# Splitting a load of weights with one instruction per engine, with rings of six places, and a bias table held for two heads at a time

## The chip, the cores and the metric

The kernel runs on one core of a Trainium2 chip. The metric is the device time of one execution in microseconds (us). The program before took 847.29, 847.55 and 848.8 us in three runs; the median is 847.55 us. Lower is better.

## What is computed

A hybrid encoder of two layers, for 256 tokens of width 1024, in float32. Of the reference, cut to what matters here:

```python
def _token_mixer(xn, w_in, w_pool, pool_scale, w_a, w_b, w_o, rel_bias):
    u, q, k, v, g_pool, g_attn = jnp.split(xn @ w_in, SPLITS, axis=-1)
    ...                                   # pooled: centred means of u minus u, by group
    pool_out = jnp.einsum('bsgc,gcd->bsgd', pooled, w_pool).reshape(B, S, POOL_WIDTH) * pool_scale
    ...
        logits = einsum(q, k) * scale + bias      # 4 heads in each of 3 groups, rel_bias by distance
        p = exp(logits - lse); o = einsum(p, v)   # the groups joined by the softmax of lse
    ...
    merged = sigmoid(g_pool) * (pool_out @ w_a) + sigmoid(g_attn) * (attn_out @ w_b)
    return merged @ w_o

def _conv_ffn(xn, w_up, conv_w, conv_b, w_down):
    a, gval = jnp.split(xn @ w_up, 2, axis=-1)
    a = conv(a) + conv_b                          # depthwise, width 3
    return (jax.nn.gelu(a) * gval) @ w_down

def reference(...):
    h = x
    for layer in range(DEPTH):
        h = h + _token_mixer(_rmsnorm(h, norm1[layer]), ...)
        h = h + _conv_ffn(_rmsnorm(h, norm2[layer]), ...)
    return _rmsnorm(h, norm_f)
```

Nearly all of the arithmetic is products of the 256 tokens with weight matrices that are read once from memory (186 MB are read in all).

## The kernel before

**Weights.** Each product of f32 operands a and w is made of three matmuls on values of a shorter mantissa (fp32r): first part of a by first part of w, first part of a by rest of w, rest of a by first part of w. So each weight is split on the chip. The class Weights does it. A *load* is one DMA of 1 MB (128 partitions x 2048 f32) on SP's queue (L178) into one of three places of `raw`. A load has two *pieces* of 128x1024. For each piece ACT casts the first part `wh` (L259) and DVE subtracts it from `raw` to give the rest `wl` (L261). wh and wl have rings of five places (BUFS = 5), one piece each; a place comes free when PE's last matmul on the piece is done. PE takes 12 matmuls of 128x512 for a piece. `get` hands PE the next piece and first opens pieces up to LOOK = 3 (4 in stretches that are ordered by hand) ahead, as far as the ring has places, and asks for further loads. Some pieces go to other tiles ("slots") or, in the first layer's start, are scaled by a gain while they are split.

**Order.** Each engine works through its instructions in the order in which they were issued. In most of the kernel that order is the one of the calls in the code, so a cast or subtraction that isn't ready holds up what was issued behind it on the same engine. SP issues the DMAs in the same manner, and a DMA that must wait for its data holds up the DMAs behind it.

**The scores.** In the middle of each layer, while PE makes the gates' and the pool's products (t_ps), the four heads hh = 0 to 3 of attention are done between them, by a table of steps (`steps`). `scores(hh)` issues PE's matmuls s_ps, then on DVE an addition of the bias with the running minimum (L1351, reads s_ps and `bt`), on ACT the exponential (L1361), on DVE the reciprocal, on ACT the scaling (L1368), on DVE two transposes (L852). The result is turned around through memory: one DMA writes it (L857, `turning`) and four DMAs read it back (L864, `turned_p`), which `W.bring_back` issues one or more steps later. `turn(hh)` splits what came back into `pth` (ACT, L1378) and `ptl` (DVE, L1379), and `weigh(hh)` issues PE's o_ps from pth, ptl and the values (L1388), followed by the parts at2 (ACT L1397, DVE L1398). `keep_gated` (DVE L1410) makes `pa` from th (ACT L1483) and t_ps. The table of steps has scores(0) at 3, bring_back and scores(1) at 4, bring_back at 5, turn(0) and scores(2) at 7, weigh(0), bring_back and turn(1) at 8, scores(3) at 9, weigh(1) at 10, turn(2) at 12, weigh(2) at 13.

**The bias.** `build_bias`, in layer 0, spreads rel_bias over distances, puts it into memory (`fd`), and reads it back with five DMAs (L559) of 256 KB into `bt`, a constant tile of 128 x 4 heads x 640 f32, where it stays for both layers.

**The products by seven.** One block of w_up in each layer, between the MLP's groups (order `BLOCK`, lines L917 for the matmuls), and in layer 1 also some of the values (order `VALUES`) are done with seven products in place of eight (Strassen's manner): the quadrants 11, 12, 21, 22 of the weight, and sums T1 to T4 of them that DVE makes in place in `raw` (L344, two instructions of 128x1024 for each sum, each issued behind the split of a half that it needs). A sum T2 needs T1 and quadrant 22, T3 needs T2, T4 needs quadrant 21. In BLOCK a "d" stands for a piece of w_down, which PE takes in between (res_ps, L715 to L717). ACT copies banks between the products: L1681 after 11, L1685 after T1 (the "fifth" product, copied from the bank that product 22 then adds to), L1688 after 22.

Of the kernel before, what the change touches and what calls it, by code (L numbers as in the profile page):

```python
# [16 lines left out]
P = 128  # L17
# [39 lines left out]
VALUES = {  # L57
# [5 lines left out]
}  # L63
SUMS = {"22": "T2", "T2": "T3", "21": "T4"}
HALVES = (slice(0, 512), slice(512, D))
# [53 lines left out]
class Weights:  # L119
# [3 lines left out]

    RAW, BUFS, LOOK = 3, 5, 3

    def __init__(self, tc, pool, idle, small):
        self.tc, self.nc, self.pool, self.idle, self.small = tc, tc.nc, pool, idle, small
        self.loads, self.pieces = [], []  # L130
        self.n_loaded, self.n_split, self.n_got = 0, 0, 0
        self.raw, self.split = {}, {}
        self.live = set()
        self.behind, self.later = (), []
        self.last, self.rests = [None, None], {}
        self.between = []
# [3 lines left out]
        self.sums = {}  # L140

    def add(self, src, shape, cuts, tag=None):

        n = len(self.loads)
        self.loads.append((src, shape, tag))
        return [(n, cut, c_shape) for cut, c_shape in cuts]

    def use(self, pieces, slots=()):
        slots = list(slots) + [None] * len(pieces)
# [58 lines left out]
    def _split(self, upto):  # L208
        nc = self.nc
        first = self.n_split  # L210
        while self.n_split < len(self.pieces):
            i = self.n_split
            n, cut, shape, slot = self.pieces[i]
            if i >= upto and (slot is None or i >= max(upto, first + 2) or i >= upto + 4 or i < 4):
                break
            if slot is None and len(self.live) == self.BUFS:
                break
            self.load(n + 1)
            with ExitStack() as queued:
                for insts, some in self.later:  # L220
                    for inst in insts if i in some else ():
                        if not self.by_hand:
                            queued.enter_context(self.tc.issue_after(inst.ins))
                for hi, lo, *_ in self.open_next():
# [12 lines left out]
    def open_next(self):  # L237


        nc, i = self.nc, self.n_split  # L240
        n, cut, shape, slot = self.pieces[i]
        if slot is None:
            self.live.add(i)
            h, l = (
                self.pool.tile([P, *shape], F32R, tag=tag, bufs=self.BUFS, name=f"{tag}{i}")
                for tag in ("wh", "wl")
            )
        else:
            tag, part, of = (*slot, 0, 1)[:3]
            if part == 0:  # L250
                self.shared = self.idle.tile([P, of, 2, *shape], F32R, tag=tag, name=f"{tag}{i}")
            h, l = self.shared[:, part, 0], self.shared[:, part, 1]
        src = cut(self.raw[n])
        self.split[i] = (h, l)
        self.n_split += 1
        if i >= self.n_scaled:
            def make(n):
                if n == 0:
                    inst = nc.scalar.copy(out=h, in_=src)  # L259
                else:  # L260
                    inst = self.rests[i] = nc.vector.tensor_sub(out=l, in0=src, in1=h.bitcast(F32))  # L261
# [17 lines left out]

        return [scaled(j) for j in range(shape[0])]  # L280
# [10 lines left out]

    def free(self, i):
        self.live.discard(i)


@with_exitstack
def encoder(ctx, tc, x, w_in, w_pool, pool_scale, w_a, w_b, w_o, norm1, norm2, w_up, conv_w,
# [32 lines left out]
    def use_block(units, made, first):  # L330
# [6 lines left out]
        def raw(name, j):  # L337
            return W.raw[made[name][0][0]][:, 2 * j : 2 * j + 2]

        def sum_later(i, name, j):  # L340

            def make():
                one, other = terms[name]
                nc.vector.tensor_sub(out=raw(name, j), in0=raw(one, j), in1=raw(other, j))  # L344

            W.sums[i] = make

        for j in range(2):
            sum_later(len(W.pieces) + first + j, "T1", j)
        behind = [u for u in units if len(u) > 2]  # L350
        for unit in units:
            if len(unit) > 2:
                W.use([unit])
                behind = behind[1:] or behind
                continue
            name, j = unit
            if name in SUMS:
                sum_later(len(W.pieces), SUMS[name], j)
            if name in ("22", "21"):
                W.use([made[name][j]])  # L360
            else:
                W.use([(behind[0][0], lambda t, name=name, j=j: raw(name, j), (2, 512))])

    def first_quadrants(w, n):
        return {
# [158 lines left out]

        return turn

    bt = const.tile([P, HPG, NT * P], F32, name="bt")

    def build_bias():

# [22 lines left out]

        fd = dram.tile([1, HPG * NT * 256], F32, name="fd")
        nc.sync.dma_start(out=fd[0].rearrange("(h e) -> h e", h=HPG), in_=fsb)
        yield
        for blk, kind in enumerate((4, 3, 1, 0, 2)):
            src = bass.AP(fd.tensor, fd.offset + kind * 256, [[1, P], [NT * 256, HPG], [1, P]])
            nc.sync.dma_start(out=bt[:, :, blk * P : (blk + 1) * P], in_=src)  # L559
        yield  # L560
# [560 lines left out]
    for l in range(DEPTH):  # L1121
# [282 lines left out]
        def keep_gated(n):  # L1404
# [362 lines left out]
```

## Time and profile before

| | |
|---|---|
| median of three runs | 847.55 us |
| the profiled execution | 848.11 us |
| its span | 846.3 us |
| PE (matmul) | 99% busy |
| DVE (VectorE) | 79% busy, 860 instructions |
| ACT (ScalarE) | 63% busy, 770 instructions |
| SP's DMAs | 147,480 packets, 212.67 MB, 76.8% of 16 engines |
| granted TensorE clock | 1.00 of full speed in the stretches shown |

The profile is of one execution. A row of a timeline gives the start and the length in us, the engine, the line of the code, the operation, what it writes and reads (names without buffer numbers), sizes, and how often it ran in a row; a bracket at the end is idle time of the engine ahead of it and what ended that. SPq is SP's DMA queue: its row is the issue of a transfer, and not the transfer itself. A row of waits gives the engine and line that waited, for what, the us in total, the number of times and the longest. A row of windows gives, for a stretch of time, the busy us of PE, PE's weight loads, DVE, ACT and POOL with the number of instructions, then the granted clock, the share of the DMA engines and the GB/s. Matmuls overlap in the rows: a 128x512 one is listed with 0.39 us while the next starts 0.227 us later.

### The profile page before, as it was taken

How to read it: one execution, taken by the hardware profiler on the slowest of the kernel's cores; microseconds unless marked ns; L12 is line 12 of the kernel's file. 1: busy time of each engine (PE TensorE's matmuls, PEld its weight loads, DVE VectorE, ACT ScalarE, POOL GpSimd, SP SyncE). 2: the span in 40 equal slices, each digit the busy share in tenths (PEclk: the TensorE clock that was granted, in tenths of full speed). 3: DMA queues.
4: the chain of work that ended last, by engine and by line, in shares of the span. 5: the costliest groups of instructions: out<-in, count | busy, mean ns of one | idle time of the engine just before them, and what ended most of it. 6: DMA issues, size and time to landing. Idle time of an engine off the chain costs nothing.

```text
span 846.3 us, 10959 instructions
## 1 busy us (share of the span) xinstructions
PE 838.7 (99%) x3889; PEld 699.3 (83%) x3889; DVE 665.5 (79%) x860; ACT 531.1 (63%) x770; POOL 35.5 (4%) x96
## 2 busy tenths in 40 slices
PE   9999999999999999999999999999999999999997
PEld 7888888888888887888888888888888888888886
DVE  6968877757767799788898997868577867998884
ACT  7744556655554776488765555577455647757883
POOL 1720000000010000000000000000000100000000
PEclk9999999999999999999999999999999999999999
DMA  8699987796759886889857669968777499768861
GB/s 305 211 304 289 317 282 251 246 282 218 233 206 302 276 275 199 256 264 316 272 185 225 222 225 316 284 235 261 247 261 269 164 308 309 227 224 275 303 218 50
DMA packets 147967, 214.02 MB, mean 253 GB/s; under 512 B 7801, under 2 KB 69185, under 8 KB 147913
## 3 DMA queue, kind: packets, MB, share of 16 engines
q1 hardware_dynamic: 147480, 212.67, 76.8%
q10 hardware_dynamic: 432, 0.66, 0.2%
q8 instruction: 30, 0.49, 0.2%
q14 instruction: 25, 0.20, 0.1%
HBM read 186.02 MB, written 27.28 MB: 252 GB/s over the span
## 4 chain that ended last, share of the span: by engine, by line
PE 90%; DMA 3%; DVE 3%; ACT 2%; issue 1%; POOL 0%; ACTq 0%; SPq 0%; DVEq 0%; POOLq 0%
PE t_ps L798 54%; PE res_ps L716 6%; PE res_ps L715 6%; PE res_ps L717 6%; PE t_ps L917 4%; PE v_ps L798 3%; DMA raw<-in_w_up_dram 3%; PE v_ps L1101 3%; PE v_ps L917 2%; PE pool_ps L702 1%; PE v_ps L1000 1%; PE o_ps L1392 1%; PE s_ps L1344 1%; ACT wh L259 1%; DVE wl L261 1%; PE s_ps L1339 1%
## 5 line engine op out<-in xcount | busy, mean ns | idle before, releaser
L261 DVE TENSOR_TENSOR wl<-raw,wh 128x1024 fp32r<-128x1024 f32 x292 | 350.9, 1219 | 92.4 <-ACT wh L259 91.7
L798 PE MATMUL t_ps<-wh,x 128*128 128x512 f32 x1280 | 401.8, 390 | 0.0
L259 ACT CAST wh<-raw 128x1024 fp32r<-128x1024 f32 x292 | 302.1, 1048 | 158.8 <-PE t_ps L798 71.2
L798 PEld LDWEIGHTS t_ps<-wh,x 128*128 128x128 f32 x1280 | 240.3, 188 | 50.0
L798 PE MATMUL t_ps<-wl,x 128*128 128x512 f32 x640 | 249.0, 389 | 0.0
L798 PEld LDWEIGHTS t_ps<-wl,x 128*128 128x128 f32 x640 | 120.2, 188 | 24.7
L715 PE MATMUL res_ps<-wh,actq 128*128 128x512 f32 (+1 forms) x184 | 70.0, 380 | 0.0
L716 PE MATMUL res_ps<-wl,actq 128*128 128x512 f32 (+1 forms) x184 | 69.8, 380 | 0.0
L717 PE MATMUL res_ps<-wh,actk 128*128 128x512 f32 (+1 forms) x184 | 69.3, 380 | 0.0
L798 PE MATMUL t_ps<-wh,po 128*128 128x512 f32 x128 | 41.4, 395 | 0.0
L715 PEld LDWEIGHTS res_ps<-wh,actq 128*128 128x128 f32 x184 | 34.6, 188 | 6.7
L716 PEld LDWEIGHTS res_ps<-wl,actq 128*128 128x128 f32 x184 | 34.6, 188 | 6.7
L717 PEld LDWEIGHTS res_ps<-wh,actk 128*128 128x128 f32 x184 | 34.6, 188 | 6.5
L1604 ACT ACTIVATE a<-zga,prm 128x256 f32<-128x256 f32 x80 | 38.9, 512 | 0.0
L592 POOL TENSOR_SCALAR ss<-ss 128x1 f32<-128x1 f32 x8 | 3.1, 386 | 764.2 <-ACT junk L585 764.2
L344 DVE TENSOR_TENSOR raw<-raw,raw 128x1024 f32<-128x1024 f32 x24 | 29.3, 1222 | 0.0
L798 PEld LDWEIGHTS t_ps<-wh,po 128*128 128x128 f32 x128 | 24.0, 188 | 4.9
L715 PE MATMUL res_ps<-wh,m 128*128 128x512 f32 (+1 forms) x72 | 26.5, 368 | 0.0
L716 PE MATMUL res_ps<-wl,m 128*128 128x512 f32 (+1 forms) x72 | 26.3, 365 | 0.0
L717 PE MATMUL res_ps<-wh,m 128*128 128x512 f32 (+1 forms) x72 | 26.0, 365 | 0.0
L1608 DVE TENSOR_TENSOR y<-y,a 128x510 f32<-128x510 f32 x22 | 14.9, 679 | 13.6 <-ACT y L1602 13.6
L798 PE MATMUL t_ps<-wl,po 128*128 128x512 f32 x64 | 24.9, 390 | 0.0
(221 smaller groups left out, 1069.6 us busy)
## 6 DMA issues: line engine op xcount, KB each, us to landing
raw<-in_w_in_dram SPq DMA_DIRECT2D x58, 1024.0 KB
raw<-in_w_up_dram SPq DMA_DIRECT2D x40, 1024.0 KB
raw<-in_w_down_dram SPq DMA_DIRECT2D x22, 1024.0 KB
crossing<-crossing SPq DMA_DIRECT2D x22, 512.0 KB
crossing<-way SPq DMA_DIRECT2D x16, 512.0 KB
raw<-in_w_a_dram SPq DMA_DIRECT2D x8, 1024.0 KB
raw<-in_w_o_dram SPq DMA_DIRECT2D x8, 1024.0 KB
zga<-crossing SPq DMA_DIRECT2D x40, 128.0 KB
```

What stands on the lines that cost most here:

```text
L259: inst = nc.scalar.copy(out=h, in_=src)
L261: inst = self.rests[i] = nc.vector.tensor_sub(out=l, in0=src, in1=h.bitcast(F32))
L344: nc.vector.tensor_sub(out=raw(name, j), in0=raw(one, j), in1=raw(other, j))
L702: nc.tensor.matmul(out, w(k), x, start=(steps is first and k == 0), stop=(steps is last and k == nk - 1), skip_group_check=turns["rest"],)
L715: nc.tensor.matmul(ps, ah, wh, start=first, stop=False, skip_group_check=on)
L716: nc.tensor.matmul(ps, ah, wl, start=False, stop=False, skip_group_check=on)
L717: nc.tensor.matmul(ps, al, wh, start=False, stop=last, skip_group_check=on)
L798: nc.tensor.matmul(ps, x2[:, 2 * n + j, part, t, :], w[:, j, :], start=(n + m == 0), stop=(n == last and m == 5),)
L917: nc.tensor.matmul(ps, operands[name](part, 2 * j + c), w[:, c, :], start=(name in ("11", "T1") and j + m == 0), stop=(j == 1 and m == 5), ...
L1101: nc.tensor.matmul(ps[t], a[:, k, t, :], w[:, j, :], start=(k + m == 0), stop=(k == KD - 1 and m == 2),)
L1604: nc.scalar.mul(out=out, in_=a, mul=row(j, c))
L1608: nc.vector.tensor_add(out=y[:, :, 1:], in0=y[:, :, 1:], in1=t["a0"][:, :, : S - 1])
```

## The change

- wh and wl become one tile each with six places. Where both pieces of a load are still to be split, two neighbouring places are free and no scaling is asked for, ACT casts both pieces with one instruction of 128x2048 (L289) and DVE subtracts with one (L290). Otherwise a piece is split alone (L311, L313). If the next two pieces are a pair without two free neighbours, the pair waits unless PE needs it in the next two calls. There are 141 such pairs.
- Both pieces of a load that belongs to a product by seven are now taken one after the other: BLOCK and VALUES are written anew so that halves of a quadrant, sum, or load of w_down stand side by side.
- A sum T is made by one subtraction of 128x2048 (L402), 12 in place of 24, issued behind the split of the second half that it needs.
- `bt` holds two heads. `load_bias(first)` reads the table for heads `first` and `first + 1` with five DMAs of 128 KB (L629). It is called with 0 when the table is built in layer 0 and at the visit ("u", 1, 2) in layer 1, and with 2 at step 5 of each layer, behind that step's bring_back. `bias_of` picks the head modulo 2.

The number of matmuls stays the same.

```diff
 BLOCK = (
-    ("11", 0), ("11", 1), "d", ("T1", 0), ("T1", 1), "d", "d", ("22", 0), ("22", 1), "d", ("T2", 0), ("T2", 1), "d",
-    ("21", 0), ("21", 1), "d", ("T3", 0), ("T3", 1), "d", "d", ("T4", 0), ("T4", 1),
+    ("11", 0), ("11", 1), "d", "d", ("T1", 0), ("T1", 1), "d", "d", ("22", 0), ("22", 1), ("T2", 0), ("T2", 1), "d", "d",
+    ("21", 0), ("21", 1), ("T3", 0), ("T3", 1), "d", "d", ("T4", 0), ("T4", 1),
 )
 VALUES = {
-    ("u", 1): (0, 1, ("11", 0), 2, ("11", 1), 3, ("T1", 0)),
+    ("u", 1): (0, 1, ("11", 0), ("11", 1), 2, 3, ("T1", 0), ("T1", 1)),
...
-    RAW, BUFS, LOOK = 3, 5, 3
+    RAW, SLOTS, LOOK = 3, 6, 3
...
+        self.slots = [pool.tile([P, self.SLOTS, 1024], F32R, tag=tag, name=tag) for tag in ("wh", "wl")]
...
-            if slot is None and len(self.live) == self.BUFS:
+            if slot is None and not self.freed:
                 break
+            count = 1
+            if self.makes_two(i):
+                if self.two_slots() is not None:
+                    count = 2
+                elif i >= self.n_got + 2:
+                    break
...
-                if i in self.sums:
-                    self.sums.pop(i)()
-            self.load(self.ahead(i))
+                for j in range(i, i + count):
+                    if j in self.sums:
+                        self.sums.pop(j)()
+            self.load(self.ahead(i + count - 1))
...
+            if count == 2:
+                h, l = (s[:, at : at + 2].rearrange("p s c -> p (s c)") for s in self.slots)
+                src = whole(self.raw[n]).rearrange("p k c -> p (k c)")
...
+                    if n == 0:
+                        return nc.scalar.copy(out=h, in_=src)
+                    inst = nc.vector.tensor_sub(out=l, in0=src, in1=h.bitcast(F32))
...
-                nc.vector.tensor_sub(out=raw(name, j), in0=raw(one, j), in1=raw(other, j))
+                nc.vector.tensor_sub(out=whole(name), in0=whole(one), in1=whole(other))
...
-    bt = const.tile([P, HPG, NT * P], F32, name="bt")
+    bt = const.tile([P, 2, NT * P], F32, name="bt")
...
+    def load_bias(first):
+
+        fd = kept_bias[0]
         for blk, kind in enumerate((4, 3, 1, 0, 2)):
-            src = bass.AP(fd.tensor, fd.offset + kind * 256, [[1, P], [NT * 256, HPG], [1, P]])
+            src = bass.AP(
+                fd.tensor, fd.offset + (first * NT + kind) * 256, [[1, P], [NT * 256, 2], [1, P]]
+            )
             nc.sync.dma_start(out=bt[:, :, blk * P : (blk + 1) * P], in_=src)
...
-        b = bt[:, hh]
+        b = bt[:, hh % 2]
...
+        else:
+            visits["u", 1, 2] = ((load_bias, 0),)
...
-            5: ((W.bring_back,),),
+            5: ((W.bring_back,), (load_bias, 2)),
```

What stands on SP's queue around the scores of layer 0, before (turning and turned_p are the way through memory of the heads' exponentials, raw a load of weights):

```order
L178 DMA raw30_1460<-in_w_a_dram 128x4x512
L864 DMA turned_p_1378<-turning_1447 32x8x128 x4
L857 DMA turning_1511<-turning_1508 128x2x512
L864 DMA turned_p_1379<-turning_1511 32x8x128 x4
L178 DMA raw31_1537<-in_w_a_dram 128x4x512
L857 DMA turning_1604<-turning_1601 128x2x512
```

And after:

```order
L184 DMA raw30_1320<-in_w_a_dram 128x4x512
L933 DMA turned_p_1246<-turning_1309 32x8x128 x4
L926 DMA turning_1371<-turning_1368 128x2x512
L933 DMA turned_p_1247<-turning_1371 32x8x128 x4
L629 DMA bt_84<-fd_538 128x2x128 x5
L184 DMA raw31_1396<-in_w_a_dram 128x4x512
```

Five reads of the bias stand behind the four reads of head 1 and ahead of the next load of weights; the addition of the bias of head 2 on DVE (L1351, after: L1422) comes behind them.

DVE in the block by seven of layer 0, before (raw51 holds T1 and then T2, raw57 is w_down, raw58 quadrant 22; L344 are the sums):

```order
L852 STREAM_TRANSPOSE crossing_2907<-t_ps_2805 128x4x4x32
L261 TENSOR_TENSOR wl110_2905<-raw51_2537,wh110_2904 128x1024
L261 TENSOR_TENSOR wl111_2921<-raw56_2723,wh111_2920 128x1024
L261 TENSOR_TENSOR wl112_2935<-raw57_2764,wh112_2934 128x1024
L261 TENSOR_TENSOR wl113_2959<-raw58_2817,wh113_2958 128x1024
L344 TENSOR_TENSOR raw51_2537<-raw58_2817,raw51_2537 128x1024
L261 TENSOR_TENSOR wl114_2971<-raw58_2817,wh114_2970 128x1024
L344 TENSOR_TENSOR raw51_2537<-raw58_2817,raw51_2537 128x1024
```

And after (L290 are pairs of rests, L402 the sums T2 and T3):

```order
L921 STREAM_TRANSPOSE crossing_2615<-t_ps_2527 128x4x4x32
L290 TENSOR_TENSOR wl_76<-raw51_2306,wh_75 128x2048
L290 TENSOR_TENSOR wl_76<-raw57_2491,wh_75 128x2048
L290 TENSOR_TENSOR wl_76<-raw58_2537,wh_75 128x2048
L402 TENSOR_TENSOR raw51_2306<-raw58_2537,raw51_2306 128x2048
L290 TENSOR_TENSOR wl_76<-raw51_2306,wh_75 128x2048
L402 TENSOR_TENSOR raw50_2304<-raw51_2306,raw50_2304 128x2048
L290 TENSOR_TENSOR wl_76<-raw59_2621,wh_75 128x2048
```

Both halves of T1's rest now stand behind the transposes, and the whole rest of quadrant 22 ahead of the whole sum T2.

ACT at the same place, before (L1681 copies the first product, L1685 the fifth):

```order
L1681 COPY t_ps_2937<-t_ps_2913 128x512
L259 CAST wh113_2958<-raw58_2817 128x1024
L259 CAST wh114_2970<-raw58_2817 128x1024
L259 CAST wh115_2981<-raw57_2764 128x1024
L1685 COPY kept_2984<-t_ps_2963 128x512
L259 CAST wh116_2999<-raw51_2537 128x1024
L259 CAST wh117_3020<-raw51_2537 128x1024
```

And after (the same copies are L1752 and L1756):

```order
L1752 COPY t_ps_2645<-t_ps_2627 128x512
L289 CAST wh_75<-raw58_2537 128x2048
L289 CAST wh_75<-raw51_2306 128x2048
L1756 COPY kept_2691<-t_ps_2677 128x512
L289 CAST wh_75<-raw59_2621 128x2048
```

The copy of the fifth product stood ahead of the casts of T2 (raw51) and stands behind that cast now.

More of the change, by code (lines that the diff above doesn't have):

```diff
@@ L140, in __init__ @@
         self.sums = {}
+        self.slots = [pool.tile([P, self.SLOTS, 1024], F32R, tag=tag, name=tag) for tag in ("wh", "wl")]
+        self.freed = {slot: slot - self.SLOTS for slot in range(self.SLOTS)}
+        self.slot_of, self.n_freed = {}, 0
     def add(self, src, shape, cuts, tag=None):
@@ L145, in add @@
         self.loads.append((src, shape, tag))
-        return [(n, cut, c_shape) for cut, c_shape in cuts]
+        if len(cuts) == 1:
+            return [(n, *cuts[0], None)]
+        whole = [lambda t: t] + [False] * (len(cuts) - 1)
+        return [(n, cut, c_shape, w) for (cut, c_shape), w in zip(cuts, whole)]
     def use(self, pieces, slots=()):
@@ L220, in _split @@
                 for insts, some in self.later:
-                    for inst in insts if i in some else ():
+                    for inst in insts if i in some or i + count - 1 in some else ():
                         if not self.by_hand:
                             queued.enter_context(self.tc.issue_after(inst.ins))
-                for hi, lo, *_ in self.open_next():
+                for hi, lo, *_ in self.open_next(count):
                     hi()
@@ L338, in raw, with whole, sum_later @@
             return W.raw[made[name][0][0]][:, 2 * j : 2 * j + 2]
-        def sum_later(i, name, j):
+        def whole(name):
+            return W.raw[made[name][0][0]]
+        def sum_later(i, name):
             def make():
                 one, other = terms[name]
-                nc.vector.tensor_sub(out=raw(name, j), in0=raw(one, j), in1=raw(other, j))
+                nc.vector.tensor_sub(out=whole(name), in0=whole(one), in1=whole(other))
             W.sums[i] = make
-        for j in range(2):
-            sum_later(len(W.pieces) + first + j, "T1", j)
+        sum_later(len(W.pieces) + first + 1, "T1")
         behind = [u for u in units if len(u) > 2]
@@ L356, in use_block @@
             name, j = unit
-            if name in SUMS:
-                sum_later(len(W.pieces), SUMS[name], j)
+            if j and name in SUMS:
+                sum_later(len(W.pieces), SUMS[name])
             if name in ("22", "21"):
@@ L361, in use_block @@
             else:
-                W.use([(behind[0][0], lambda t, name=name, j=j: raw(name, j), (2, 512))])
+                W.use([(
+                    behind[0][0], lambda t, name=name, j=j: raw(name, j), (2, 512),
+                    False if j else lambda t, name=name: whole(name),
+                )])
     def first_quadrants(w, n):
```

47 lines of the change are left out of this document (38 added, 9 removed), and 8 rows, old and new, of the table VALUES.

## The prediction

> **What bounds the kernel now.** I read the page first, for the engine that is never idle, then the waits of PE, then the timelines of DVE, ACT, SP and PE at the two stages where the change puts something in front of work that PE waits for. The profiled execution took 848.11 us for a span of 846.3 us, so 1.8 us lie outside the span; it is 0.56 us over the median of the runs, 847.55 us.
>
> ```profile
> span 846.3 us, 10959 instructions
> ...
> PE 838.7 (99%) x3889; PEld 699.3 (83%) x3889; DVE 665.5 (79%) x860; ACT 531.1 (63%) x770; POOL 35.5 (4%) x96
> ```
>
> The groups of the splits and of the sums (busy us, mean ns of one, idle before them):
>
> ```profile
> L261 DVE TENSOR_TENSOR wl<-raw,wh 128x1024 fp32r<-128x1024 f32 x292 | 350.9, 1219 | 92.4 <-ACT wh L259 91.7
> ```
>
> ```profile
> L259 ACT CAST wh<-raw 128x1024 fp32r<-128x1024 f32 x292 | 302.1, 1048 | 158.8 <-PE t_ps L798 71.2
> ```
>
> PE is busy for 99% of the span, while DVE and ACT rest in front of these very splits (92.4 and 158.8 us). So splits are not the bound; they matter only where a first part or rest comes after the matmul that wants it. PE's list of waits says how much of that there is:
>
> ```profile
> PE warm_ps L502 <- PEq L1749: 0.8, 1, 0.8
> PE t_ps L917 <- DVE crossing L852: 0.4, 1, 0.4
> PE xt_ps L627 <- DVE xn L618: 0.3, 1, 0.3
> ```
>
> The longest stretch of the chain that ended last gives PE's pace, 70.80 us for 312 matmuls or 0.227 each:
>
> ```profile
> 41.06 70.80 PE t_ps L798 x312
> ```
>
> Three waits, 1.5 us, of which the first is the start. Quicker DVE and ACT can take off no more than the other 0.7 us, 0.1% of the time, and a measurement of this kernel can tell about 0.2% (1.7 us) from no change. So the question is what the change can add.
>
> **The change part by part.** *Price of a pair.* Back to back, four rests take 4.59 us and one takes 1.22 (rows below), so each next one costs 1.12. A 128x512 subtraction takes 0.68 (the ptl row) and a 128x1024 one 1.22: 0.54 for each 512 elements, hence 128x2048 about 2.3 us, against 2.34 for two. For ACT 1.05 a cast, and 0.61 for the 128x512 cast at 165.23: 0.44 for each 512, a pair 1.93. So a pair saves DVE and ACT some 0.1 us, 14 us each over 141 pairs, off the path: worth nothing. In exchange the first piece of a pair, and whatever stands behind it on its engine, comes later: one ACT cast (0.9 us) and one DVE subtraction (1.1 us).
>
> *Where there is cover.* With six places and pairs, most casts may start four pieces (4 x 12 matmuls x 0.227 us = 10.9 us) ahead of use and need 1.9 + 2.3; in the values of layer 1 and the residuals I count two to three pieces, 5.4 to 8.2 us. There I put the change at nothing; what is lost if the cover fails is about 1 us a place. The T sums of 128x2048 likewise. Two places lack cover.
>
> *Bias table.* DVE, ACT, SP and PE about the second to fourth heads of layer 0 (start, length, line, operation):
>
> ```profile
> 149.96 1.04 ACT L259 CAST wh<-raw 128x1024 fp32r<-128x1024 f32 x1
> ```
>
> ```profile
> 164.02 1.03 ACT L259 CAST wh<-raw 128x1024 fp32r<-128x1024 f32 x1
> 164.96 0.37 ACT L1397 ACTIVATE at<-o_ps 128x256 fp32r<-128x256 f32 x1
> 165.23 0.61 ACT L1378 CAST pth<-turned_p 128x512 fp32r<-128x512 f32 x1
> ```
>
> ```profile
> 152.17 0.68 DVE L1351 CUSTOM_DVE_ANT_0 s<-s_ps,bt 128x512 f32<-128x512 f32 x1
> ```
>
> ```profile
> 160.64 0.68 DVE L1351 CUSTOM_DVE_ANT_0 s<-s_ps,bt 128x512 f32<-128x512 f32 x1
> ...
> 166.23 0.42 DVE L1398 SCALAR_TENSOR_TENSOR at<-o_ps,at 128x256 fp32r<-128x256 f32 x1
> 166.56 0.68 DVE L1379 TENSOR_TENSOR ptl<-turned_p,pth 128x512 fp32r<-128x512 f32 x1
> ...
> 168.43 0.69 DVE L1351 CUSTOM_DVE_ANT_0 s<-s_ps,bt 128x512 f32<-128x512 f32 x1
> ...
> 171.49 1.32 DVE L852 STREAM_TRANSPOSE turning<-p 128x512 f32<-128x512 f32 x2 [0.45 <-ACT p L1368]
> 172.74 1.25 DVE L1410 SCALAR_TENSOR_TENSOR pa<-th,t_ps 128x512 f32<-128x512 f32 x2
> ```
>
> ```profile
> 156.42 0.38 SPq L857 DMA_DIRECT2D turning<-turning  x1
> 160.49 1.78 SPq L864 DMA_DIRECT2D turned_p<-turning  x4
> 162.37 0.40 SPq L178 DMA_DIRECT2D raw<-in_w_a_dram  x1
> ```
>
> ```profile
>   L559 SPq DMA_DIRECT2D bt<-fd x5: 366/508/2216, 48.9 to 51.2; - x5
> ```
>
> ```profile
> 161.25:163.75 2.50, 2.50 (x15) 2.17 (x14) 1.24 (x7) 2.38 (x6) 0.00 (x0) 1.00 0.96 224
> ```
>
> ```profile
> 171.91 0.29 PE L1388 MATMUL o_ps<-ptl,vh 128*128 128x256 f32 x1
> ```
>
> ```profile
> 181.72 0.28 PE L1388 MATMUL o_ps<-ptl,vh 128*128 128x256 f32 x1
> ```
>
> The heads 2 and 3 of the table can be loaded only when scores(1) has read head 1, and on SP the five issues stand behind the write and the four reads of turning(1). First, scores(1) is later: its rest is now a pair, whose cast starts at 149.96, so 149.96 + 1.93 + 2.3 = 154.1 in place of 152.17, 1.9 later. The write goes from 156.42 to 158.3. From write to reads 4.07 us here (3.77 in layer 1): reads at 162.1 to 162.4, for 1.78; then five issues at 0.37 to 0.51 us: last out at 165.8 to 166.8. The reads before, last issue out at 162.27, were through at 163.75 (the window row: 0.96 of the DMA engines until then), 1.5 after. So the table lands at B = 167.3 to 168.3; I allow 0.5 us more below, for a quicker turning, and take 167.5. DVE, which came to scores(2) at 160.64 and would now come at about 162, waits 5 us, and everything on DVE and, through the exponentials, on ACT stands behind it: the raw30 pair, at2 of head 0, ptl and pth of head 1. From scores(2) on: 164.02 - 160.64 = 3.4 until the cast, 1.9 cast, 2.3 rest, 0.33 at2 (166.23 to 166.56), 0.7 ptl: B + 8.6 = 176.1. PE wanted that ptl at 171.91: it waits **4.2 us**. Next, scores(3) begins at that moment: 3.1 to its transposes (168.43 to 171.49), 1.25, 1.2 for pa, then pairs raw31 and raw32 with at2 between (2.2 + 0.3 + 2.3) and ptl 0.7: 11.0, where PE needs 181.72 - 171.91 = 9.8. **1.2 more** (0 to 1.9, since raw32 also waits on ACT for th). Head 3 has 2 us of slack. Layer 1 has the same order:
>
> ```profile
> 572.62 0.38 SPq L857 DMA_DIRECT2D turning<-turning  x1
> 576.39 1.93 SPq L864 DMA_DIRECT2D turned_p<-turning  x4
> ```
>
> ```profile
> 588.12 0.28 PE L1388 MATMUL o_ps<-ptl,vh 128*128 128x256 f32 x1
> ```
>
> 572.62 + 1.9 + 3.77 + 1.93 + 2.2 + 1.5 = 583.9; + 8.6 - 588.12 = **4.4**, and 1.2. Sum of the bias: 5.4 + 5.6 = 11.0 us; from its bounds 7 to 13.6. The trace has no DMA that lands in front of scores(2); "nothing" is a rival below. By the Trainium skill ("DMA: Bandwidth & Descriptors", Latency and other measured facts) a DMA has a fixed cost of about 2 us, mostly the receipt; with 2 us in place of 1.5 after the last issue the sum would be 12.0. No row here separates that receipt from data still moving, so the 1.5 of the row stands.
>
> *MLP block* (L344, L917), in layer 0; what DVE, PE and ACT did:
>
> ```profile
> 317.18 1.30 DVE L852 STREAM_TRANSPOSE crossing<-t_ps 128x512 f32<-128x512 f32 x2
> 318.41 4.59 DVE L261 TENSOR_TENSOR wl<-raw,wh 128x1024 fp32r<-128x1024 f32 x4
> ```
>
> ```profile
> 317.24 0.39 PE L717 MATMUL res_ps<-wh,actk 128*128 128x512 f32 x1
> 318.03 0.47 PE L917 MATMUL t_ps<-wh,sx 128*128 128x512 f32 x1 [0.41 <-DVE crossing L852]
> ```
>
> ```profile
> 322.29 0.58 ACT L1685 COPY kept<-t_ps 128x512 f32<-128x512 f32 x1
> 324.24 1.05 ACT L259 CAST wh<-raw 128x1024 fp32r<-128x1024 f32 x1 [1.37 <-DVE raw L344]
> ```
>
> The wait at 317.24 (0.57 over the 0.227 pace) goes, since a d now stands ahead of T1: -0.6. After it T1 runs 320.2 to 322.9 and two d until 328.35. DVE from 318.41: rests of T1, d, 22 (3 x 2.24) until 325.1, the whole T2 sum until 327.4; only then can ACT cast T2 until 329.3, and the copy of the fifth product (L1685), which frees the bank that product 22 writes, now stands behind that cast: 329.9, product 22 comes **1.5 us** late. Before, the copy stood ahead of the wait for the sum. Then the rest of the next d: T2's rest, T3 sum, d's rest, 3 x 2.25 from 329.3 = 336.1, wanted at 329.9 + 2 x 2.72 + 0.2 = 335.5: **0.6**. T1's own rest, 320.7, wanted at 320.4: 0.3. Layer 0: -0.6 + 2.4 = 1.8; layer 1, where the list shows no such wait, less by its somewhat earlier start, 1.0. Sum 2.8, bounds 1 to 4.
>
> Total: 848.1 + 11.0 + 2.8 = 861.9 for an execution like the profiled one, less 0.56: **861.3 us**.
>
> **The rivals.** *Half clock after the long waits.* Waits of 4.2 us would leave the PE clock gated; in place of 0.227 the matmuls behind take twice that. For one piece of 12, 2.72 us more, at one wait in each layer: 866.7. For it: no wait over 0.8 us is in this trace, so nothing shows the clock holding. Against: it is 1.00 in the window row, and only waits longer than any here would do it. The Trainium skill ("TensorE: Matmul & The Clock Gate", Part 1: The HAM clock gate) has the clock halve after an idle window of about 3.4 us and come back after as long a busy one. By that rule the price would be 1.7 us a wait, and it strikes only if the wait covers a whole window. Chance 0.10.
>
> *The table lands in time.* If SP passed the turning faster, so that B is at most 171.91 - 8.6 = 163.3, DVE would lose nothing PE sees. That is sooner than the five issues can even be out by the sum above, so it would take reads that leave 4 us earlier than their write allows. Only the block remains: 847.55 + 2.8 = 850.3. Chance 0.08.
>
> *Not slower: nothing reaches PE.* Decisive is the order in which ACT and DVE are asked: if the copy of the fifth product or the T2 cast has 1.5 us more cover than I count and the table 4 us, then PE stays at 99% and only the waits at 317.24 and near the start of layer 1 go, 0.7 us: 846.9, or 847.5 where they stay. For it: DVE and ACT rest 250 us in front of splits in all. Against: those rests lie elsewhere: from 317.18 to 323.0 the two DVE rows of the block stand back to back, and at 155 to 165 it is the DMA that DVE would wait for. Chance 0.14.
>
> **How the numbers follow.** Forecast 0.68, half clock 0.10, table in time 0.08, nothing reaches PE 0.14. The forecast's own bounds: 847.55 + 7 + 1 = 855.6 to 847.55 + 13.6 + 4 + 1 (a place without cover) = 866. The range reaches down to the table in time and up to the half clock: 850 to 867, leaving out the last rival. That one splits into 0.04 faster by over 0.2% and 0.10 within; slower is 0.86.
>
> **What would show it.** PE's waits should list o_ps (by DVE ptl) twice in each layer, about 4 and 1 us, with DVE's scores line waiting for a DMA into bt some 5 us. In the block PE should wait for the ACT copy of the fifth product, about 1.5 us, and the wait for the crossing of layer 0 should be gone. PE's busy time stays at 838 to 840 us and its clock at 1.00; a clock under that after the waits is the first rival. Wrong I am if DVE shows no wait for bt, or if that wait is there and o_ps doesn't follow it.

## The result and the profile after

The changed kernel takes 879.31 us (median of four runs, 878.44 to 880.54) against 847.53 us before: a ratio of 1.037 with a 95% interval of 1.036 to 1.039, 31.8 us slower. The forecast was slower by 13.8, with a range that ended at 867. The profiled execution has a span of 877.5 us, 31.2 more than before, and its page reads:

```profile
span 877.5 us, 10610 instructions
...
PE 849.3 (97%) x3889; PEld 703.3 (80%) x3889; DVE 654.4 (75%) x707; ACT 511.0 (58%) x629; POOL 36.4 (4%) x96
```

DVE and ACT have 153 and 141 instructions less and are busy 11 and 20 us less. The 31 us are PE's: it is busy 10.6 us longer for the same 3889 matmuls, and idle for the rest. What it waits for (in total, times, longest):

```profile
PE o_ps L1459 <- DVE ptl L1450: 7.5, 4, 2.1
PE o_ps L1459 <- ACT pth L1449: 5.3, 3, 2.2
PE s_ps L1410 <- DVE nm L1422: 2.3, 2, 2.1
PE xt_ps L696 <- DVE xn L687: 2.0, 4, 0.9
PE t_ps L986 <- ACT kept L1756: 1.8, 2, 0.9
```

So the waits for head 1 and for the copy of the fifth product are there, as forecast, but o_ps waits seven times and not four, and it begins with head 0. DVE around the bias additions (L1422) of layer 0, which stood at 152.17, 160.64 and 168.43 us for heads 1, 2 and 3 before:

```profile
150.46 0.69 DVE L1422 CUSTOM_DVE_ANT_0 s<-s_ps,bt 128x512 f32<-128x512 f32 x1
...
158.94 0.68 DVE L1422 CUSTOM_DVE_ANT_0 s<-s_ps,bt 128x512 f32<-128x512 f32 x1
...
173.57 0.69 DVE L1422 CUSTOM_DVE_ANT_0 s<-s_ps,bt 128x512 f32<-128x512 f32 x1 [6.43 <-PE t_ps L867]
174.19 0.08 DVE L1422 DVE_READ_ACCUMULATOR2_ANT nm<- 128x1 f32 x1
174.84 0.69 DVE L1422 CUSTOM_DVE_ANT_1 s<-s_ps,bt 128x512 f32<-128x512 f32 x1 [0.57 <-DMA bt<-fd]
...
182.04 0.68 DVE L1450 TENSOR_TENSOR ptl<-turned_p,pth 128x512 fp32r<-128x512 f32 x1
```

These are heads 0, 1 and 2. Head 1 is at 158.94, 6.8 us late, where 1.9 was forecast, and head 2 at 173.57, 12.9 late. (The wait at 173.57 is put down to a matmul of t_ps, but the matmuls that this addition reads, s_ps, ran from 159.54 to 161.30; what it lacks is the table. Its first half reads the blocks of the first four DMAs; its second half reads that of the fifth too, and begins 1.3 us later.) SP at that place:

```profile
163.19 0.38 SPq L926 DMA_DIRECT2D turning<-turning  x1
166.11 1.78 SPq L933 DMA_DIRECT2D turned_p<-turning  x4
167.94 2.50 SPq L629 DMA_DIRECT2D bt<-fd  x5
```

The order is the forecast one and 4 to 5 us late; and the table, whose last issue ends at 170.44, lands at 174.8, 4.4 after it, where 1.5 was taken.

Why head 0 is late stands further up in the queue. SP before, and then after, at the end of the keys:

```profile
126.27 1.80 SPq L864 DMA_DIRECT2D way<-crossing  x4
128.17 0.40 SPq L178 DMA_DIRECT2D raw<-in_w_a_dram  x1
133.72 0.38 SPq L857 DMA_DIRECT2D crossing<-way  x1
136.52 1.80 SPq L864 DMA_DIRECT2D kz<-crossing  x4
```

```profile
125.60 2.05 SPq L933 DMA_DIRECT2D way<-crossing  x4
134.88 0.38 SPq L926 DMA_DIRECT2D crossing<-way  x1
137.62 1.79 SPq L933 DMA_DIRECT2D kz<-crossing  x4
139.52 0.40 SPq L184 DMA_DIRECT2D raw<-in_w_a_dram  x1
```

The load raw27 is asked for when the first piece of raw25 is split; with a pair that is only after both pieces, which comes behind the next crossing in the order. So it goes out at 139.52 in place of 128.17, behind a write and four reads that wait for it. Its pair is split ahead of the first bias addition on both engines:

```profile
146.31 1.91 ACT L289 CAST wh<-raw 128x2048 fp32r<-128x2048 f32 x1 [5.52 <-DMA raw<-in_w_a_dram]
```

```profile
148.25 2.29 DVE L290 TENSOR_TENSOR wl<-raw,wh 128x2048 fp32r<-128x2048 f32 x1 [5.44 <-ACT wh L289]
```

ACT and DVE stand still for 5.5 us, and the softmax of head 0 behind them. In layer 1 the load raw102 slips in the same way, from 544.26 to 572.58, behind the reads of kz at 570.39.

Last, PE's clock (a stretch of time, PE, PEld, DVE, ACT, POOL, then the granted clock):

```profile
168.00:170.50 2.50, 2.50 (x12) 2.40 (x11) 0.00 (x0) 0.00 (x0) 0.00 (x0) 0.50 0.79 194
184.00:187.50 3.50, 3.50 (x14) 3.11 (x14) 2.30 (x6) 3.50 (x7) 0.00 (x0) 0.50 0.65 143
614.30:617.50 3.20, 3.06 (x14) 2.98 (x15) 1.94 (x8) 2.48 (x6) 0.00 (x0) 0.58 1.11 318
```

Half clock stands behind three of the four groups of waits of o_ps. It lasts 3.4, 6.8 and 3.4 us (167.67 to 171.08, 181.33 to 188.15 and 614.82 to 618.23); PE is busy for 12.2 us of that, so by an estimate half of it, 6.1 us, is what the clock costs. The block is as forecast; PE there:

```profile
344.41 0.50 PE L986 MATMUL t_ps<-wh,sx 128*128 128x512 f32 x1 [0.91 <-ACT kept L1756]
...
350.67 0.50 PE L785 MATMUL res_ps<-wl,actq 128*128 128x512 f32 x1 [0.29 <-DVE wl L290]
```

### The profile page after: what moved, and what is told of

Its sections match the earlier page's. It is cut to its first block, busy times and chain, and to the rows that moved or that the text cites. A ratio compares the mean times of both kernels' runs of the same rounds, so it can differ in the third digit from the quotient of the medians.

```text
span 877.5 us, 10610 instructions
## 1 busy us (share of the span) xinstructions
PE 849.3 (97%) x3889; PEld 703.3 (80%) x3889; DVE 654.4 (75%) x707; ACT 511.0 (58%) x629; POOL 36.4 (4%) x96
## 4 chain that ended last, share of the span: by engine, by line
PE 56%; DVE 13%; ACT 12%; DMA 9%; issue 6%; SPq 2%; POOL 0%; ACTq 0%; DVEq 0%; POOLq 0%
PE t_ps L867 38%; ACT wh L289 7%; DVE wl L290 7%; PE v_ps L867 3%; DMA raw<-in_w_up_dram 3%; PE v_ps L1170 2%; PE v_ps L986 2%; DMA raw<-in_w_in_dram 2%; PE t_ps L986 2%; PE res_ps L785 1%; PE res_ps L786 1%; DMA raw<-in_w_a_dram 1%; PE res_ps L784 1%; PE v_ps L1069 1%; SPq L933 1%
## 5 line engine op out<-in xcount | busy, mean ns | idle before, releaser
L290 DVE TENSOR_TENSOR wl<-raw,wh 128x2048 fp32r<-128x2048 f32 x141 | 321.7, 2287 | 129.0 <-ACT wh L289 127.5
L289 ACT CAST wh<-raw 128x2048 fp32r<-128x2048 f32 x141 | 268.6, 1909 | 161.4 <-PE t_ps L867 83.0
L1432 ACT ACTIVATE p<-s,nm 128x512 f32<-128x512 f32 x16 | 11.5, 717 | 36.1 <-DVE nm L1422 35.5
L402 DVE TENSOR_TENSOR raw<-raw,raw 128x2048 f32<-128x2048 f32 x12 | 27.4, 2286 | 0.0
L921 DVE STREAM_TRANSPOSE way<-t_ps 128x512 f32<-128x512 f32 x32 | 21.5, 699 | 4.9 <-PE t_ps L867 4.9
```

What stands on the lines that cost most here:

```text
L289: return nc.scalar.copy(out=h, in_=src)
L290: inst = nc.vector.tensor_sub(out=l, in0=src, in1=h.bitcast(F32))
L402: nc.vector.tensor_sub(out=whole(name), in0=whole(one), in1=whole(other))
L921: nc.vector.transpose(out=y.rearrange("p q c j -> p c q j"), in_=rows)
L1432: nc.scalar.activation(p, s, AF.Exp, bias=nm[:, 0:1], scale=-1.0, accum_out=z)
```

## The experiments

The theory that the traces suggest (S): the late load raw27 and the reload of the table hold the same queue of DVE one after the other, and half clock follows. Its rivals: the reload alone is nearly all (Q); the pairs themselves cost it (P). All ratios are to the kernel before on the same chip.

**The table alone.** The kernel before, with the hunks of the change for `bt`, `load_bias` and `bias_of` and nothing else:

```diff
-    bt = const.tile([P, HPG, NT * P], F32, name="bt")
+    bt = const.tile([P, 2, NT * P], F32, name="bt")
...
-            5: ((W.bring_back,),),
+            5: ((W.bring_back,), (load_bias, 2)),
```

> The kernel before with only the two-head bias table and its reloads; single splits, old block order. Theory S (two causes in series: in the changed kernel the load of weights raw27, issued behind the reads of kz, holds head 0 some 5 us, and the reload of the bias table holds head 2; both hold the same queue of DVE, and PE's clock halves for some 3.4 us after long waits): here raw27 is in its old place, so scores(0) stays near 145.5 us and only the reload acts; with the landing 3.6 to 4.4 us behind the last issue that the changed kernel shows, head 2's addition starts near 169, PE waits 3 to 4 us for ptl of head 1 in each layer, with or without 1.7 us of half clock behind it: 855 to 859. Theory Q (the reload alone is nearly all): 870 or more. Theory P (the pairs in front of the scores are the cause, the reload hides): within 1 us of 847.5.

Measured: 860.1 us, 1.014 (1.013 to 1.016). 1.1 us above S's upper end, and far from the times of P and Q, which both fall. The reload costs 12 us by itself, with single splits and raw27 in its old place.

**No reload.** The changed kernel with step 5 and the visit of layer 1 as before:

```diff
-        else:
-            visits["u", 1, 2] = ((load_bias, 0),)
...
-            5: ((W.bring_back,), (load_bias, 2)),
+            5: ((W.bring_back,),),
```

> The changed kernel without the three reloads of the bias table behind the first, so that heads 2 and 3 get the biases of heads 0 and 1 in both layers (part of the computation is changed). Theory S: head 0 is still 5 us late, PE waits for pth and ptl of head 0 (3.2 us and half clock behind it in layer 0, 2.3 in layer 1), and the wait for head 1 goes: 858 to 864. Theory Q: 850 to 853. Theory P: 860 to 870, with waits wherever pairs stand ahead of the scores.

Measured: 862.84 us, 1.018 (1.014 to 1.021). S, against Q: without any reload 15 us remain. P's range holds this time too; what speaks for S is that PE waits for head 0 (3.5 us in layer 0, 1.7 in layer 1). Two of the four executions took 860.3 and 860.8 us at a mean granted clock of 0.999, the other two 864.9 and 866.5 at 0.994 and 0.995: whether the clock halves behind such a wait differs from one execution to the next.

**The loads in their old place.** In `_split`, after the load ahead:

```diff
             self.load(self.ahead(i + count - 1))
+            if count == 2 and n in (24, 99):
+                self.load(self.ahead(i + count))
```

> The changed kernel with the loads raw27 and raw102 issued where the kernel before has them, ahead of the crossing and of the reads of kz; nothing else. Theory S: scores(0) is back to within 1 us of 145.5, the waits for head 0 go, the reload still holds head 2 until about 170 and PE waits 6 to 7 us for head 1 with half clock behind it: 864 to 871. Theory Q: no gain, 877 to 880. Theory P: no gain either, 876 to 880, since the pairs stay.

Measured: 871.51 us, 1.027 (1.025 to 1.029), 7.8 less than the change. S. Moving two DMAs in SP's queue, and nothing else, brings head 1's addition to 155.0. The reload still holds head 2; SP, and then DVE:

```profile
163.80 2.51 SPq L631 DMA_DIRECT2D bt<-fd  x5
```

```profile
169.65 0.69 DVE L1424 CUSTOM_DVE_ANT_0 s<-s_ps,bt 128x512 f32<-128x512 f32 x1 [6.44 <-DMA bt<-fd]
...
171.28 0.69 DVE L1424 CUSTOM_DVE_ANT_1 s<-s_ps,bt 128x512 f32<-128x512 f32 x1 [0.93 <-DMA bt<-fd]
```

The issues begin at 163.80, as the prediction has it (162.1 to 162.4 and 1.78 later); the table is whole at 171.28, 5.0 us after the last issue.

**Both.** The two edits above together.

> The changed kernel without the reloads (heads 2 and 3 get the biases of heads 0 and 1) and with raw27 and raw102 issued in their old place. Theory S: no wait of o_ps is left, PE's clock stays at 1.00 throughout; what is left are the waits of the block for the copy of the fifth product (1.1 and 1.1 us) and for the rest (0.45 twice) and the waits for xn: 849.5 to 852. Theory Q: the same as without the reloads, and the earlier loads add nothing to it. Theory P: 858 or more.

Measured: 857.44 us, 1.012 (1.010 to 1.013). No theory had that: the waits of o_ps are gone as S said, but 9 us are left where S left 1 to 4. So P has a part.

**The reload ahead of the turning.** With the loads in their old place, and in `scores`:

```diff
             y = sm.tile([P, 2, 4, 4, 32], F32, tag="gain", bufs=1, name="turning")
+            if hh == 1:
+                load_bias(2)
             cross(ps, y, turned_z[hh % 2], "turning")
...
-            5: ((W.bring_back,), (load_bias, 2)),
+            5: ((W.bring_back,),),
```

> The changed kernel with raw27 and raw102 in their old place and the reload for heads 2 and 3 issued as soon as head 1 has read its biases, ahead of the write of turning(1) in SP's queue; everything is computed. Theory S (only the place of the reload costs): it lands some 7 us before scores(2) asks, no wait of o_ps is left, the time is that of the run without reloads and with early loads, 856 to 859. Theory L (the reload costs wherever it stands, since its 1280 small packets and five issues hold the turning of head 1 by 2.5 us or more): PE still waits for head 1, 861 to 866.

Measured: 857.02 us, 1.010 (1.009 to 1.012). The same bytes, packets and issues, two places earlier in SP's queue, cost nothing: it is the place of the reload and not the reload.

**The two calls swapped.** With the loads in their old place, step 5 asks for the reload ahead of the reads:

```diff
-            5: ((W.bring_back,), (load_bias, 2)),
+            5: ((load_bias, 2), (W.bring_back,)),
```

> The run with early loads, and step 5 calls the reload first and bring_back second, so that the five issues stand between the write and the reads of turning(1), in the time in which SP waits for the write; everything is computed. Theory S: the issues begin near 159.7 in place of 163.8, the table lands near 166, PE's wait for head 1 is about 2 us in each layer, 859 to 863. Rival (the packets of the reload slow the turning's own way through memory by as much): 867 or more.

Measured: 864.27 us, 1.017 (1.014 to 1.021). Half way: the table is there at 168.2, but the issues (161.36 to 164.22) hold back the reads of turning(1) by some 0.6 us (3.4 us after the write, 2.7 in the run with early loads). The median is 1.3 us above S's range; the interval takes in its upper end and doesn't reach the rival's.

**One DMA in place of five.**

```diff
         fd = kept_bias[0]
+        if first:
+            src = bass.AP(fd.tensor, fd.offset + first * NT * 256, [[1, P], [NT * 256, 2], [1, NT * P]])
+            nc.sync.dma_start(out=bt, in_=src)
+            return
```

> The run with early loads (raw27 and raw102 in their old place), in which the reload for heads 2 and 3 is one DMA of the same 640 KB with packets of 2560 bytes in place of five with packets of 512; the table's blocks then hold other entries, so heads 2 and 3 get wrong biases. In the run with early loads the second addition of head 2 began 5.0 us after the end of the last issue. Theory K (five issues, 2.5 us, and 1280 small packets make the table late): it lands some 4 us earlier, PE's wait for head 1 shrinks to 2 to 4 us without half clock behind it, 861 to 866. Theory M (the load of weights right behind it, or the receipt, makes it late): it lands at most the 2 us of the issues earlier, 867 to 870.

Measured: 869.23 us, 1.024 (1.021 to 1.027): the time of theory M, whose cause holds only in part. SP, and then DVE:

```profile
163.58 0.45 SPq L629 DMA_DIRECT2D bt<-fd  x1
164.13 0.41 SPq L184 DMA_DIRECT2D raw<-in_w_a_dram  x1
```

```profile
169.72 0.69 DVE L1428 CUSTOM_DVE_ANT_0 s<-s_ps,bt 128x512 f32<-128x512 f32 x1 [7.02 <-DMA bt<-fd]
```

The issue ends at 164.03, and the 640 KB are there 5.7 us later, with the load of weights now issued right behind. The last issue ends 2.3 us earlier than in the run with early loads and the table is whole 1.6 us earlier, so five issues and small packets cost no more than that. How far the load behind shares the engines, the run with early loads shows. Its packets from the end of the last issue (166.31) to the first half of the addition (169.65), and from there to the second half (171.28):

```profile
DMA packets 1139, 0.63 MB, mean 188 GB/s; under 512 B 69, under 2 KB 1087, under 8 KB 1139
...
DMA packets 302, 0.60 MB, mean 370 GB/s; under 512 B 2, under 2 KB 9, under 8 KB 302
```

The packets of the load are those of 2 KB, 52 in the first stretch and 293 in the second. So the table is late mostly by its own moving, 3.3 us for the first four blocks with hardly a packet of the load; only the few last packets of the fifth block run among the load's, 1.6 us more. In the swapped run, where the load comes 2.6 us later and the four reads stand between, the table still needs 4 us. How much is sharing in the run with one DMA stays open.

**The copy first.** The reload ahead, and T2's pair is opened one step later:

```diff
             count = 1
+            if i in self.hold and i >= self.n_got + 3:
+                break
...
+            if name == "T2" and len(units) == len(BLOCK):
+                W.hold.add(len(W.pieces))
```

> The run with the reload ahead, and in the MLP block the pair T2 is opened one step later, so that ACT copies the fifth product ahead of T2's cast; nothing else. Theory S: PE's wait for that copy, 0.9 us in each layer (1.07 over the pace), goes, and if T2's rest is still in time the time falls by 1.5 to 2.2 us, to about 855. Rival: the wait moves to T2's rest or to the rests of the d behind it, and the time stays within 0.7 us.

Measured: 857.11 us, 1.012 (1.009 to 1.015), no difference: the rival. The wait for the copy goes, and the rests of the d behind make up for it (0.6 us in two waits before the edit):

```profile
PE res_ps L792 <- DVE wl L295: 2.7, 2, 1.3
```

In the block the copy's place was the wait that ended last and not the cause: the whole of T2's cast, T2's rest, T3's sum and d's rest in a row is too long for what PE has ahead of it.

**Singles, with the reload ahead.** `makes_two` gives False; rings of six places, new orders and whole sums stay:

```diff
-        if i < self.n_scaled or i + 1 >= len(self.pieces):
-            return False
+        return False
```

> The run with the reload ahead, but every piece is split alone (rings of six places, new orders, whole sums). Theory S: the some 9 us that are left are mostly later first halves of pairs, in front of xn and in the block: 849 to 852. Rival (the new orders of the block and the values and the whole sums cost it): 855 to 858.

Measured: 850.28 us, 1.003 (1.001 to 1.004). So S holds for the reload and P for most of what was left: 6.7 us of the 9 are the pairs' own. PE's waits with pairs and the reload ahead, and then with singles:

```profile
PE xt_ps L698 <- DVE xn L689: 2.2, 4, 0.9
PE t_ps L988 <- ACT kept L1760: 1.8, 2, 0.9
...
PE res_ps L787 <- DVE wl L292: 0.6, 2, 0.3
```

```profile
PE xt_ps L697 <- DVE xn L688: 1.6, 3, 1.0
...
PE t_ps L987 <- ACT kept L1759: 0.3, 1, 0.3
```

The block's waits nearly vanish, though it has the new order and whole sums. The waits for xn shrink less (0.3 us in the kernel before), so a part of them comes with the rings or orders and not with the pairs. The lists name some 3 us of the 6.7. Matmul beside matmul, the two profiled executions part by 7.2 us: 3.1 in the two blocks, 2.2 around the two norms behind the MLPs, and the rest in steps of 0.2 to 0.4.

**Singles alone.** The changed kernel with the same edit of `makes_two`, the reload where the change has it:

> The changed kernel in which every piece is split alone and nothing else is altered: the reload is where the change puts it, the rings have six places, the new orders and whole sums stay; by its order of issue raw27 and raw102 are back ahead of the crossing without being moved. Theory S: the cost of the reload with singles (some 12 us, from the kernel before with the table alone) and the 2 to 3 us of the orders add: 860 to 864; so the pairs bring 15 to 19 of the 31 us, 8 of them by the late load, 7 by their own first halves, the rest by making the reload dearer. Rival (late load comes from the new rings and orders, not from pairs): 868 or more.

Measured: 862.07 us, 1.016 (1.012 to 1.020). S: the order of issue puts raw27 and raw102 back by itself, so the late load is a result of the pairs.

**The clock by itself.** A program of its own, run once; this is the core of its code. `hold(n)` makes PE wait for n additions on DVE, then `dense` issues matmuls:

```python
        dense(DENSE, ps)
        for n in PLAN:
            for m in n if isinstance(n, tuple) else (n,):
                hold(m, ps)
                ps = pp.tile([P, 512], F32, name="dense_ps")
                dense(1, ps)
            dense(DENSE, ps)
```

> Not the encoder: a program of 65 matmuls of 128x512 at a time, between which PE waits for a chain of 0 to 9 subtractions-like additions of 128x512 on DVE (0.6 us each, so waits of some 0.5 to 6 us in mixed order), and some with one matmul between two waits; the output is zeros. Theory G (the clock is halved when PE has been idle for a whole window of about 3.4 us on a grid of its own): no half clock after waits under 3.4 us, always after waits over 6.8, sometimes between; half clock lasts about 3.4 us, costing 1.7 us. Rival: half clock after every wait over about 2 us, and none after two waits with a matmul between.

Some of its rows: start, length of the 65 matmuls, and in the bracket the wait ahead of them:

```profile
38.57 16.62 PE L39 MATMUL dense_ps<-a,w 128*128 128x512 f32 x65 [2.77 <-DVE a L45]
...
79.90 15.02 PE L39 MATMUL dense_ps<-a,w 128*128 128x512 f32 x65 [2.04 <-DVE a L45]
...
202.57 0.47 PE L39 MATMUL dense_ps<-a,w 128*128 128x512 f32 x1 [2.04 <-DVE a L45]
205.08 16.62 PE L39 MATMUL dense_ps<-a,w 128*128 128x512 f32 x65 [2.04 <-DVE a L45]
...
460.03 15.01 PE L39 MATMUL dense_ps<-a,w 128*128 128x512 f32 x65 [3.50 <-DVE a L45]
```

Undisturbed, 65 take 15.0 us. After single waits of 0.57, 1.32 and 2.04 us (four) they take that; after 2.77 (three) 16.6; of four waits of 3.50 one left the clock whole; from 4.22 on all lost 1.3 to 2.9 us. Two waits of 2.04 with one matmul between lose 1.6 as well, both times; two of 1.32 nothing. The rival fails on the two waits in a row and on the wait of 3.50.

The changes of the clock show the grid: in every trace that has several, they lie whole multiples of 3.41 us apart. Some windows of that grid in this program (behind the stretch come its length and PE's busy time; the granted clock is the third number from the end):

```profile
35.16:38.57 3.41, 0.64 (x3) 0.22 (x2) 2.45 (x5) 0.00 (x0) 0.00 (x0) 1.00 0.00 0
38.58:41.99 3.41, 3.41 (x8) 2.73 (x9) 0.00 (x0) 0.00 (x0) 0.00 (x0) 0.50 0.00 0
...
202.42:205.83 3.41, 1.22 (x4) 0.86 (x5) 1.76 (x5) 0.00 (x0) 0.00 (x0) 1.00 0.00 0
205.83:209.24 3.41, 3.41 (x9) 2.65 (x8) 0.00 (x0) 0.00 (x0) 0.00 (x0) 0.50 0.00 0
...
455.00:458.41 3.41, 1.53 (x7) 0.94 (x5) 1.74 (x4) 0.00 (x0) 0.00 (x0) 1.00 0.00 0
458.42:461.83 3.41, 1.80 (x8) 1.53 (x9) 1.39 (x3) 0.00 (x0) 0.00 (x0) 1.00 0.00 0
461.83:465.24 3.41, 3.41 (x17) 2.81 (x16) 0.00 (x0) 0.00 (x0) 0.00 (x0) 1.00 0.00 0
```

A wait of 2.77 us leaves PE busy for 0.64 us of a window, two of 2.04 us for 1.22, and half clock follows both. The wait of 3.50 us that left the clock whole lies across two windows, with PE busy for 1.53 and 1.80. Over all thirteen traces half clock followed every window in which PE was busy for less than 1.4 us and none with more than 1.7; between them both occur. So theory G has the grid right, and is wrong in that a window must be idle throughout.

## Why the prediction was wrong

Laid one on the other, the runs give 31 us step by step, by their medians: 848.0 before; 850.3 with rings of six, new orders and whole sums (the singles); 857.0 with pairs; 871.5 with the reload where the change puts it; 879.3 with raw27 and raw102 late. That is 2.3 + 6.7 + 14.5 + 7.8 (by the ratios, each on its own chip: 2.2, 6.5, 14.4 and 8.5).

- *What bounds the kernel:* right. PE was at 99%, quicker DVE and ACT gained nothing, all of it is waits that were added.
- *Price of a pair:* right. 2287 and 1909 ns are measured, 2.3 and 1.93 us were worked out.
- *The step that failed first:* "With six places and pairs, most casts may start four pieces [...] ahead of use". That was counted in places of wh and wl. The order of SP was read only from the scores on, and a few rows above it a load stood in another place. A pair delays the split of its first piece and with it the load that is issued behind that split; here it fell behind a crossing that waits for PE. 7.8 us, which no rival held. The row of the new order was there to be read.
- *Where there is cover, "I put the change at nothing":* 6.7 us, of which the block's 2 to 3 were forecast under their own head.
- *Bias:* the mechanism was right, the size wrong. 11.0 forecast, 14.5 measured with raw27 in place. The mis-sized term is the 1.5 us from the last issue to the landing, read from turned_p: 4.4 us in the changed kernel, 5.0 with early loads, where the table moves at 122 to 205 GB/s (165 to 169 us) and turned_p had 224 in the prediction's row. With the 2 us of the Trainium skill ("DMA: Bandwidth & Descriptors", Latency and other measured facts) in its place the sum is 12.0, hardly nearer. Against this, the 1.2 us for ptl of head 2 came neither in the changed kernel nor with early loads, and PE meets the late table at three places, s_ps, pth and ptl of head 1. The listed waits there add up to 9.7 us with early loads, so it isn't they that pass the 11.0 but the half clock behind them, some 6.4 us in that trace by the same estimate. (Why the two together come to more than 14.5 stays open.) With singles the reload costs 11 to 12 us, near the forecast; there the clock halves at the scores for 3.4 us in all (the table alone) or not at all (singles alone).
- *Half clock:* it came, at 0.10 as a rival of its own and not as part of the sum, which holds it at nothing. At three places it costs some 6.1 us in the changed kernel, within the 14.5 and 7.8; the rival had 5.4 for it. I had held against it that "only waits longer than any here would do it", and forecast such waits of 4.2 us in the same text.
- *Block:* right. The waits for the copy (0.91 listed of the first one) and for the rest of d (0.29) are the forecast ones with 1.5 and 0.6, if smaller, and the wait for the crossing is gone. That the copy's place causes it was argued and falls with the run that moves it.

No version beat the kernel before; the best, the singles with the reload ahead, is 0.3% behind it. The change takes instructions from engines that had time, and takes away slack, which they hadn't.

## What to carry to other kernels

When instructions are merged, follow not only the two that become one: read the new order of every queue whose issues hang on them, from the first row that moved, and ask for each DMA that has slipped behind a waiting one who needs it. A transfer is best issued when its buffer comes free, ahead of the next one on the queue that must wait; the same reload cost 14.5 us at one place and nothing two rows above. Price a wait of PE of more than some 2 us, or two shorter ones close together, with the half clock that can follow.

## What the runs showed of the hardware

PE's clock changes on a grid of 3.41 us. In the thirteen traces it fell to half behind every window of that grid in which PE was busy for less than 1.4 us and behind none with more than 1.7. So one wait of 2.77 us was enough (three of three), or two of 2.04 us with one matmul of 0.47 between, and one of 3.50 us across two windows was not; after single waits of up to 2.04 us the clock stayed whole (four of four; the two of 2.04 us each lay across two windows). In the program by itself each fall cost 1.3 to 2.9 us. The Trainium skill ("TensorE: Matmul & The Clock Gate", Part 1: The HAM clock gate) has the clock fall after an idle window of about 3.4 us, and the window run freely. The grid in the traces agrees; that the window must be idle doesn't, and here the measurement decides.

A transfer of 640 KB needed 4.0 to 5.7 us in layer 0 from the end of its last issue until DVE could read it, whether in 1280 packets of 512 bytes or 256 of 2560. The Trainium skill ("DMA: Bandwidth & Descriptors", Latency and other measured facts) states a fixed cost of about 2 us, mostly the receipt and more where the memory is busy. In the run with early loads no packet under 2 KB, so none of the table, moves from 170.83 on, and DVE begins at 171.28: of the 5.0 us no more than 0.45 lie behind the moving of the data.
